# The second image of the late pairs leaves by GpSimd's queue

## The chip, the core and the metric

The kernel runs on one core of a Trainium2 chip. Its time is device microseconds of one execution. A profile is one execution recorded by the hardware profiler; its span runs from the first instruction to the last, on one clock for all engines.

## What is computed

A 3x3 convolution with dilation 2 and zero padding over 16 images of 64 channels and 64x64 pixels, to 128 channels, in float32. The reference, cut to its core:

```python
batch, c_in, h, w, c_out, k, dilation = 16, 64, 64, 64, 128, 3, 2
pad = ((k - 1) * dilation + 1) // 2
x_pad = np.pad(x, ((0, 0), (0, 0), (pad, pad), (pad, pad)))
output[b, co] += weight[co, ci, kh, kw] * x_pad[b, ci, kh*dilation:kh*dilation+h, kw*dilation:kw*dilation+w]
```

An image comes in as 1.05 MB of float32 and goes out as 2.10 MB.

## The kernel before

**Pairs.** The images are worked two at a time. `x_pair` puts the 64 channels of both images of a pair on the 128 partitions, so a pair is one load of 2.10 MB. There are `NP` = 8 pairs, `pb` = 0 to 7. The output tile `o` of a pair holds 128 output channels on the partitions and both images beside each other, 4.19 MB.

**Loads.** Pair 0 comes as float32 by SyncE's queue (L75) into a tile from the pool of the output tiles, and is cast to f16 by the engines. Pairs 1 to 7 are loaded by `load` (L81) on GpSimd's queue, which casts to f16 on the way: 2.10 MB are read, 1.05 MB written. Pairs 1 to 4 are asked for at the start. Pairs 5, 6 and 7 are asked for in the loop over pairs, two pairs ahead (L195, `AHEAD` = 5).

**Sums.** The kernel spares matmuls by working rows that lie two apart together: of four rows (`e`, `r`), rows with `e` = 0 and `e` = 1 share the middle tap, which is applied to their sum. `prepare` (L141) makes these sums `s16` on GpSimd, in two pieces for each pair: at the second and the third step (`u` = 1, 2) of the pair before. The pool of sums has three buffers, so GpSimd waits until PE has read the sums of three pairs earlier.

**Matmuls.** Each pair has `NU` = 4 steps `u` of 16 output rows. A step has three phases, each in its own PSUM tile (four buffers): the middle tap on the sums, copied to `s32` by ScalarE (L204), and one phase for each `e`, which VectorE (DVE) adds to `s32` into `o` (L209).

**Stores.** The pool of output tiles has three buffers, and its first one serves pair 0's float32 load, so the tile of pair `pb` takes the buffer of pair `pb` - 3, and DVE's first add of a pair waits until the store of that pair has landed. All stores leave by SyncE's queue (SP): pairs 0 to 4 as one DMA of 4.19 MB (L221), pairs 5 and 6 as one DMA for each image (L224), and pair 7 in two halves of rows with one DMA for each image. Each store waits for DVE's last add into what it takes.

**Order.** The schedule is written by hand: every engine and every queue keeps the order of the code. An instruction of GpSimd that waits holds all that stands behind it on GpSimd, sums and DMA requests alike.

Of the kernel before, what the change touches and what calls it, by code (L numbers as in the profile page):

```python
# [10 lines left out]
def kernel(  # L11
# [7 lines left out]
    nc = tc.nc  # L19

    B, CI, H, W = x.shape
# [8 lines left out]
    NP = B // 2  # L30
# [47 lines left out]
    def load(pb, cuts):  # L78
        x16[pb] = x16pool.tile([P, H, W], f16, tag="x16", name=f"x16_{pb}")
        for lo, hi in zip(cuts, cuts[1:]):  # L80
            nc.gpsimd.dma_start(out=x16[pb][:, lo:hi], in_=x_pair[pb, :, lo:hi])  # L81

    AHEAD = 5
# [16 lines left out]
    for name, a in (("w21", 2), ("w01", 0)):  # L100
        for u in range(2):
            eng = nc.vector if name == "w21" else nc.gpsimd
            eng.tensor_sub(  # L103
                out=w16[:, SLOT[name] * KW : (SLOT[name] + 1) * KW, u, :],
# [8 lines left out]
    for n, name in enumerate(("w1", "w21", "w0", "w01", "w2")):  # L113
        ps = cpool.tile([P, 2, NB], f32, tag="ps", name=f"wt{n}")
        k0 = SLOT[name] * KW
        for j in range(KW):
            nc.tensor.matmul(  # L117
                out=ps[:, 0, j * CO : (j + 1) * CO],
# [16 lines left out]
    def prepare(pb, lo, hi):  # L135
        if pb not in s16:
            s16[pb] = sumpool.tile([P, 2 * NQ, W], f16, tag="s16", name=f"s16_{pb}")
        src = (x16[pb] if pb else x32).rearrange("p (q e r) w -> p q e (r w)", e=2, r=2)
        dst = s16[pb].rearrange("p (q r) w -> p q (r w)", r=2)
        q0, q1 = lo // 4, hi // 4  # L140
        nc.gpsimd.tensor_add(  # L141
            out=dst[:, q0:q1], in0=src[:, q0:q1, 0, :], in1=src[:, q0:q1, 1, :]
        )
# [37 lines left out]
    def phase(pb, u, terms):  # L181

        ps = cpool.tile([CO, 2, NB], f32, tag="ps", name="ps")
        for pair in zip(*(conv(pb, hb, ps[:, hb], u, terms) for hb in range(2))):
            for m in pair:
                nc.tensor.matmul(**m)  # L186
        return ps

    BOTH = NP - 3
    for pb in range(NP):  # L190
        o = opool.tile([P, 2, H, W], f32, tag="o", name=f"o{pb}")
        ov = o.rearrange("p b (q e r) w -> p b q e (r w)", e=2, r=2)
        for u in range(NU):

            if u == 1 and AHEAD <= pb + 2 < NP:  # L195
                load(pb + 2, [0, H])
            if pb + 1 < NP:
                if u == 1:
                    prepare(pb + 1, 0, 36)
                elif u == 2:  # L200
                    prepare(pb + 1, 36, H)

            s32 = spool.tile([P, 2, NB], f32, tag="s32", name="s32")
            nc.scalar.copy(out=s32, in_=phase(pb, u, [("w1", 2, 0)]))  # L204
            for e, terms in enumerate(
                ([("w21", 1, 0), ("w0", 1, -1)], [("w01", 0, 0), ("w2", 0, 1)])
            ):
                ps = phase(pb, u, terms)
                nc.vector.tensor_add(  # L209
                    out=ov[:, :, u * UQ : (u + 1) * UQ, e, :],  # L210
                    in0=ps.rearrange("p b (q c) -> p b q c", c=QW),
                    in1=s32.rearrange("p b (q c) -> p b q c", c=QW),
                )

            step = NU // 2 if pb == NP - 1 else NU
            if (u + 1) % step == 0:
                fl = slice((u + 1 - step) * 4 * UQ, (u + 1) * 4 * UQ)
                if pb < BOTH:  # L220
                    nc.sync.dma_start(out=out_pair[pb], in_=o)  # L221
                else:
                    for hb in range(2):
                        nc.sync.dma_start(out=out[2 * pb + hb, :, fl], in_=o[:, hb, fl])  # L224


# [33 lines left out]
```

## Time and profile before

| | |
|---|---|
| time, median of 3 runs | 126.64 us (126.16 to 126.73) |
| span of the profiled execution | 124.3 us |
| own device time of the profiled execution | not listed beside its span; the median is 2.3 us over the span |
| PE busy | 105.2 us, last matmul ends before 111 us |
| DVE, ScalarE, GpSimd busy | 80.8, 39.6, 41.4 us |
| moved by the DMA engines | 43.42 MB, mean 349 GB/s |
| HBM read, written | 17.07 MB, 33.55 MB |
| stores, issue to last landing (median) | 21.6 us (4.19 MB), 12.4 us (2.10 MB), 10.6 us (1.05 MB) |
| loads by GpSimd's queue, issue to last landing (median) | 16.0 us |

The page gives the busy time of each engine in 40 slices of the span (3.1 us each), as a digit of tenths; the line DMA is the mean share of the core's 16 DMA engines, and GB/s what they moved, counted as written. q1 is SyncE's queue, q0 GpSimd's. A timeline's line gives the start, the time taken, engine, line, operation and how many; in brackets stands how long the engine was idle before it and what ended that. A line of the stretches gives each engine's busy time and number of instructions, then the granted clock, the DMA share and GB/s.

### The profile page before, as it was taken

The numbers are of one execution on the slowest core, as the hardware profiler recorded it, in microseconds if no ns is written. First come the engines' busy times: TensorE is split into PE (matmuls) and PEld (weight loads), VectorE is DVE, ScalarE is ACT, GpSimd is POOL, SyncE is SP. The second block draws the span as 40 slices with busy tenths as digits, with TensorE's granted clock in tenths as the row PEclk, the third lists the DMA queues.
The fourth block names the chain that finished last, engine by engine and source line by source line (L and its number), as shares of the span: only waits on it lengthen the run. The fifth ranks groups of instructions, "written<-read, shape, count | busy, mean of one in ns | idle before, by whom it ended". The sixth has DMA issues, their size and how long they took to land.

```text
span 124.3 us, 2244 instructions
## 1 busy us (share of the span) xinstructions
PE 105.2 (85%) x981; PEld 55.7 (45%) x981; DVE 80.8 (65%) x71; ACT 39.6 (32%) x40; POOL 41.4 (33%) x33
## 2 busy tenths in 40 slices
PE   6357999999999999999999999999999999960000
PEld 2043555555555555555555555555555555520000
DVE  0470199787778777877769778777877787770000
ACT  4760823333333333333333333333332433320000
POOL 2859998794095009500930093000000000000000
PEclk9999999999999999999999999999999999999655
DMA  4999999999999999999999999999999999999991
GB/s 129 346 359 218 214 214 216 224 237 411 393 327 314 332 306 319 316 390 314 324 345 427 425 427 432 422 427 427 432 438 427 432 414 432 427 417 419 422 406 71
DMA packets 3961, 43.42 MB, mean 349 GB/s; under 512 B 368, under 2 KB 368, under 8 KB 624
## 3 DMA queue, kind: packets, MB, share of 16 engines
q1 hardware_dynamic: 2944, 35.95, 68.9%
q0 software_dynamic: 1008, 7.34, 28.4%
q8 instruction: 7, 0.11, 0.3%
q14 instruction: 2, 0.02, 0.0%
HBM read 17.07 MB, written 33.55 MB: 407 GB/s over the span
## 4 chain that ended last, share of the span: by engine, by line
PE 80%; DMA 5%; POOL 2%; DVE 1%; DVEq 1%; SPq 0%; issue 0%
PE ps L186 80%; DMA x<-in_x_dram 5%; POOL s L141 2%; DVE o L209 1%; DVEq L255 1%; SPq L64 0%; DVEq L209 0%
## 5 line engine op out<-in xcount | busy, mean ns | idle before, releaser
L209 DVE TENSOR_TENSOR o<-ps,s 128x1024 f32<-128x1024 f32 x64 | 76.7, 1223 | 25.9 <-PE ps L186 16.8
L186 PE MATMUL ps<-x,w_sb 64*128 64x496 f16 (+3 forms) x768 | 85.3, 368 | 0.0
L186 PEld LDWEIGHTS <-w_sb 64*128 64x128 f16 x960 | 53.4, 95 | 49.3 <-issue 3.7
L204 ACT COPY s<-ps 128x1024 f32<-128x1024 f32 x32 | 32.4, 1012 | 63.0 <-PE ps L186 63.0
L141 POOL TENSOR_TENSOR s<-x 128x1152 f16<-128x1152 f16 (+4 forms) x18 | 35.1, 1971 | 31.1 <-PE ps L186 28.3
L186 PE MATMUL ps<-s,w_sb 64*128 64x496 f16 (+1 forms) x192 | 26.5, 379 | 2.1 <-POOL s L141 2.1
L81 POOL DMA_DIRECT2D x<-in_x_dram x7 | 4.0, 579 | 0.0
L132 ACT CAST x<-x 128x1024 f16<-128x1024 f32 (+1 forms) x3 | 2.8, 973 | 3.4 <-DMA x<-in_x_dram 3.4
L93 PE MATMUL warm<-zero 128*128 128x512 f16 x6 | 2.7, 630 | 1.2 <-DVE zero L87 1.2
L117 PE MATMUL wt<-ident,w 128*128 128x128 f16 x15 | 1.8, 312 | 2.1 <-ACT w L99 2.1
L103 DVE TENSOR_TENSOR w<-w 128x192 f16<-128x192 f32 x2 | 1.5, 800 | 2.5 <-DMA w<-in_weight_dram 2.5
L117 PEld LDWEIGHTS <-w 128*128 128x128 f16 x15 | 1.5, 146 | 3.0 <-ACT w L99 3.0
L99 ACT CAST w<-w 128x576 f16<-128x576 f32 x2 | 2.3, 1222 | 1.6 <-DMA w<-in_weight_dram 1.6
L103 POOL TENSOR_TENSOR w<-w 128x192 f16<-128x192 f32 x2 | 1.9, 951 | 2.4 <-DMA w<-in_weight_dram 2.4
L126 DVE CAST w_sb<-wt 128x384 f16<-128x384 f32 x3 | 1.6, 552 | 1.4 <-PE wt L117 1.4
L93 PEld LDWEIGHTS <-zero 128*128 128x128 f16 x6 | 0.7, 138 | 2.3 <-DVE zero L87 1.2
L99 ACT ACT_TABLE_LOAD x1 | 1.3, 1283 | 0.7 <-PEq L241 0.7
L128 ACT CAST w_sb<-wt 128x384 f16<-128x384 f32 x2 | 1.0, 478 | 1.1 <-PE wt L117 1.1
L130 DVE CAST x<-x 128x1280 f16<-128x1280 f32 x1 | 0.8, 826 | 0.5 <-DMA x<-in_x_dram 0.5
L87 DVE MEMSET zero<- 128x256 uint32 x1 | 0.3, 272 | 0.9 <-PEq L241 0.9
masks.py:199 POOL TENSOR_SCALAR_AFFINE_SELECT ident<-ident 128x128 f16<-128x128 f16 x1 | 0.3, 292 | 0.1
masks.py:197 POOL MEMSET ident<- 128x128 f16 x1 | 0.2, 204 | 0.3 <-POOLq L241 0.3
(4 smaller groups left out, 0.4 us busy)
## 6 DMA issues: line engine op xcount, KB each, us to landing
out_dram<-o SPq DMA_DIRECT2D x5, 4096.0 KB, 21.6
out_dram<-o SPq DMA_DIRECT2D x4, 2048.0 KB, 12.4
x<-in_x_dram POOLq DMA_DIRECT2D x7, 1024.0 KB, 16.0
out_dram<-o SPq DMA_DIRECT2D x4, 1024.0 KB, 10.6
x<-in_x_dram SPq DMA_DIRECT2D x1, 1152.0 KB, 6.5
x<-in_x_dram SPq DMA_DIRECT2D x1, 896.0 KB, 10.6
w<-in_weight_dram SPq DMA_DIRECT2D x1, 288.0 KB, 2.9
```

What stands on the lines that cost most here:

```text
L81: nc.gpsimd.dma_start(out=x16[pb][:, lo:hi], in_=x_pair[pb, :, lo:hi])
L93: nc.tensor.matmul(out=warm[:, 0], lhsT=zero[:, 0:P], rhs=zero, start=True, stop=True)
L99: nc.scalar.copy(out=w16[:, 0:NK, u, :], in_=w32k)
L103: eng.tensor_sub(out=w16[:, SLOT[name] * KW : (SLOT[name] + 1) * KW, u, :], in0=w32k[:, a * KW : (a + 1) * KW, :], in1=w32k[:, KW : 2 * KW ...
L117: nc.tensor.matmul(out=ps[:, 0, j * CO : (j + 1) * CO], lhsT=w16[:, k0 + j, :, :].rearrange("o t i -> o (t i)"), rhs=ident, start=True, st ...
L126: nc.vector.tensor_copy(out=dst, in_=ps[:, 0, 0 : KW * CO])
L132: nc.scalar.copy(out=x16[0][:, lo:hi], in_=x32[:, lo:hi])
L141: nc.gpsimd.tensor_add(out=dst[:, q0:q1], in0=src[:, q0:q1, 0, :], in1=src[:, q0:q1, 1, :])
L186: nc.tensor.matmul(**m)
L204: nc.scalar.copy(out=s32, in_=phase(pb, u, [("w1", 2, 0)]))
L209: nc.vector.tensor_add(out=ov[:, :, u * UQ : (u + 1) * UQ, e, :], in0=ps.rearrange("p b (q c) -> p b q c", c=QW), in1=s32.rearrange("p b ( ...
L255: with _tile.TileContext(nc) as tc:
```

## The change

Pair 4 (the fifth) leaves as two DMAs, one for each image, as pairs 5 to 7 do. Of each such two, the first image's DMA stays on SyncE's queue, and the second's goes to GpSimd's. The load of pair 7 is taken out of its place in pair 5 and asked for in pair 4, behind the sums for pair 5.

```diff
-    BOTH = NP - 3
+    PAIRED = NP - 4
     for pb in range(NP):
...
-            if u == 1 and AHEAD <= pb + 2 < NP:
+            if u == 1 and AHEAD <= pb + 2 < NP - 1:
                 load(pb + 2, [0, H])
             if pb + 1 < NP:
                 if u == 1:
                     prepare(pb + 1, 0, 36)
                 elif u == 2:
                     prepare(pb + 1, 36, H)
+                    if pb == PAIRED:
+                        load(NP - 1, [0, H])
...
-                if pb < BOTH:
+                if pb < PAIRED:
                     nc.sync.dma_start(out=out_pair[pb], in_=o)
                 else:
-                    for hb in range(2):
-                        nc.sync.dma_start(out=out[2 * pb + hb, :, fl], in_=o[:, hb, fl])
+                    for hb, eng in enumerate((nc.sync, nc.gpsimd)):
+                        eng.dma_start(out=out[2 * pb + hb, :, fl], in_=o[:, hb, fl])
```

GpSimd's order from the sums of pair 5 on, before: load of pair 7, sums of pair 6, sums of pair 7. After: load of pair 7, store of pair 4's second image, sums of pair 6, store of pair 5's, sums of pair 7, store of pair 6's, two stores of pair 7's. The number of instructions on PE, DVE and ScalarE is the same.

## The prediction, made before the changed kernel ran

> **What bounds the kernel now.** I read the page's slices first, because the chain of waits ends at 112.01 us (1.13 us of DVE's own queue after 110.88) while the span ends at 124.3 us. Whatever fills the last 12 us is not in that chain.
>
> ```profile
> PE   6357999999999999999999999999999999960000
> ...
> DMA  4999999999999999999999999999999999999991
> GB/s 129 346 359 218 214 214 216 224 237 411 393 327 314 332 306 319 316 390 314 324 345 427 425 427 432 422 427 427 432 438 427 432 414 432 427 417 419 422 406 71
> ...
> q1 hardware_dynamic: 2944, 35.95, 68.9%
> q0 software_dynamic: 1008, 7.34, 28.4%
> ```
>
> PE looks full for most of the span, but it stops three slices before the end. The DMA engines are at 9 in every slice except the first and the last. So the transfers set the end. The low GB/s figures in slices 4 to 20 are the loads: they write f16 and read twice as many bytes, which the next view, by stretches, lets me compare.
>
> ```profile
> core 0: us, PE busy (x) PEld busy (x) DVE busy (x) ACT busy (x) POOL busy (x), PEclk, DMA share, GB/s
> 14.00:24.00 10.00, 10.00 (x100) 5.42 (x97) 7.98 (x7) 4.03 (x5) 9.30 (x5) 1.00 1.02 214
> 36.00:48.00 12.00, 12.00 (x120) 6.37 (x118) 9.19 (x9) 4.05 (x4) 4.35 (x4) 1.00 1.01 315
> 76.00:112.00 36.00, 34.66 (x336) 18.20 (x332) 28.30 (x24) 11.13 (x11) 0.00 (x0) 1.00 1.01 429
> 118.00:120.00 2.00, 0.00 (x0) 0.00 (x0) 0.00 (x0) 0.00 (x0) 0.00 (x0) 0.50 1.03 434
> 120.00:122.00 2.00, 0.00 (x0) 0.00 (x0) 0.00 (x0) 0.00 (x0) 0.00 (x0) 0.50 0.68 287
> 122.00:124.00 2.00, 0.00 (x0) 0.00 (x0) 0.00 (x0) 0.00 (x0) 0.00 (x0) 0.50 0.05 20
> ```
>
> From 14 to 24 us only GpSimd's queue (q0) moves data: 214 GB/s written, so 428 GB/s read. From 76 to 112 only SyncE's queue (q1) does: 429 GB/s. From 36 to 48 both do; the DMA view of that stretch gives 1.27 MB for q0 and 2.49 MB for q1, so 2.54 + 2.49 MB at the f32 side in 12 us, 419 GB/s, and 48 to 60 gives 434. One queue, the other, or both: the engines move the f32 side at the same pace. An image of 2.10 MB costs 2.10 MB / 429 GB/s = 4.9 us of all sixteen engines, whoever asks for it.
>
> That gives the whole time. In the trace's landing records (one time for each of the sixteen engines) the second piece of x's first pair lands from 8.6 to 12.3 us. After it come 7 loads and 16 images out, 23 x 4.87 us = 112.0 us. For the fastest engine 8.6 + 112.0 = 120.6, and its last landing is at 120.9; the slowest lands at 123.4, and the span closes 0.9 us later. So the fastest engine idles for 0.3 us in 112, and that is all that better order can take, except for the uneven finish (120.9 to 123.4).
>
> **The change part by part.** Now the queues' own clocks, from the timelines of SP and GpSimd:
>
> ```profile
> 74.93 0.37 SPq L221 DMA_DIRECT2D out_dram<-o  x1
> 87.30 1.51 SPq L224 DMA_DIRECT2D out_dram<-o  x2
> 112.04 1.63 SPq L224 DMA_DIRECT2D out_dram<-o  x2
> ...
> 50.73 0.57 POOL L81 DMA_DIRECT2D x<-in_x_dram  x1
> 58.95 4.21 POOL L141 TENSOR_TENSOR s<-x 128x1152 f16<-128x1152 f16 x2 [7.65 <-PE ps L186]
> 71.31 4.21 POOL L141 TENSOR_TENSOR s<-x 128x1152 f16<-128x1152 f16 x2 [8.14 <-PE ps L186]
> ```
>
> *The eighth pair's load.* Before, it stands on GpSimd behind both sums of pair 5 and ahead of the sums of pair 6, and leaves at 50.73. After, it stands in the same place in GpSimd's order, with the new store behind it. Cost 0. Had it stayed at its place in the loop, it would stand behind a store that waits until 74.9.
>
> *One DMA more.* The fifth pair (pair 4 counted from 0) leaves as two DMAs and not one: 16 more completion packets (the page's 368 under 512 B are 16 for each of 23 issues), one per engine, some 10 ns each in the packet records. Cost 0.01 us.
>
> *SP.* It loses one issue of each later group. The second issue of a group takes 1.1 to 1.4 us (1.51 to 1.75 for the two). Nothing gains by it: a store issued at 87.30 lands after some 11 to 16 us, of which its own transfer is 4.9; it stands in the engines' backlog. Gain 0.
>
> *GpSimd.* It gains five store issues at 0.54 to 0.70 us each (the loads' durations; I take 0.57, the median of L81). What is queued behind each matters. The first waits for DVE at 74.93, and the sums of pair 6, which ran at 58.95, now run from 75.5 to 79.7. PE first reads them at 85.74: cover 6.0 us. The second waits until 87.30, and the sums of pair 7, which ran at 71.31, end at 87.30 + 0.57 + 4.21 = 92.1. PE first reads them at 98.11: cover 6.0 us. Cost 0; without that cover each would hold PE.
>
> On whether GpSimd can write its store requests while DVE is busy: the load at 50.73 took 0.57 us with a DVE add running (50.65 to 53.09), the three loads at 9.84 took 0.54 to 0.57 with DVE nearly idle. So DVE's adds cost such a request nothing. The Trainium skill (SBUF — State Buffer, section SBUF: two separate sides) says that a DVE operation in a two-port mode keeps GpSimd from writing descriptors until it ends. By that rule a store would be late by at most one add, 1.22 us, which the 6.0 us cover; these rows show no such hold.
>
> *Who lands when.* At 74.93 SP's queue still has all of pair 3 (landing before at 62.56 + 21.6 = 84.2). The new store of pair 4's second image shares the engines with it from then on, so pair 3 lands 4.87 us later, at 89.0, or 89.4 if the next store (87.3) cuts in. Pair 6's output tile is pair 3's buffer, and DVE first writes it at 87.76: a wait of some 1.6 us. The trace has one such wait:
>
> ```profile
> DVE o L209 <- DMA out_dram<-o: 1.2, 1, 1.2
> ...
> 63.76 4.87 DVE L209 TENSOR_TENSOR o<-ps,s 128x1024 f32<-128x1024 f32 x4 [1.23 <-DMA out_dram<-o]
> ```
>
> After it DVE ran four adds without a gap, PE never stopped, and the next adds came at 69.37, on the regular grid. DVE's gap is 0.75 us in each 3.17, so 1.6 us are made up in about 7 us, inside pair 6's 12.4. Then pair 4's first image, behind pair 3 and beside two stores of the other queue, lands at 84.2 + 3 x 4.87 = 98.8 (before: 74.93 + 18.9 = 93.8); pair 7 first writes that buffer at 100.13. Cover 1.3 us. If it is gone, DVE is late by what is missing, and the end is not: at 112.04, when the last stores are issued, the engines are busy with earlier ones until 115.9 (fastest) to 118.5 (slowest). The start of a DMA takes about 1.6 us (weights: issued 0.74, first landing 3.01, 0.7 of it transfer), so the fastest engine has 2.3 us of cover, the slowest 4.9.
>
> *The end.* From 98.8 on q1 holds 3 images and q0 2, in all 5 x 4.87 = 24.35 us: 123.15 against 123.4 before. q0 is through at about 120.5 and q1's last half image goes alone, as now.
>
> *What a store costs by q0.* The trace has none. Nearest are q0's loads: 8 packets per engine, 4.87 us per 2.10 MB read, the same as q1's stores (96.4 to 101.3 for an image). I take the same. From below: nothing in the rows lets a packet go faster, 0. From above: if rows of 16 KB were cut in pieces of 4 KB (from 309 ns for 8 KB and 611 for 16 KB a packet has some 7 ns of its own, so 4 KB takes 158), 4 x 158 = 632 against 611, +3.4% on 4 x 4.87 us, or +0.7 us. The loads' bytes written give a far bound, 214 GB/s: another 19.5 us; but those packets read 16 KB each, and that explains their time.
>
> Sum: 0 + 0.01 + 0 = 0 on a span of 124.3 us. The profiled execution's own device time is not listed beside its span; the median of the runs, 126.64, lies 2.3 us over the span, and I keep that. Forecast 126.6 us. About 0.5% (0.63 us) is what a measurement of this kernel can tell from no change.
>
> **The rivals.** *Slower: the sixteen engines lose time on q0's stores.* Engines are full, so each lost percent of q0's 19.5 us goes straight to the end; it decides from +3.3% per packet on (0.63 us). Against it: the equal pace of loads and mixed stretches. For it: no store by this queue is in the trace, and in 24 to 31 us, with q1's first store coming in, the slowest engine's landings of two successive loads are 24.4 and 30.7, 6.2 us apart and not 4.9, 1.35 more. Priced from 0.7 (cut rows) to 4 x 1.35 = 5.4 us; I take 1.5: 128.1. The Trainium skill (DMA: Bandwidth & Descriptors, section Latency and other measured facts) calls two of the sixteen engines usually slower, and guesses at GpSimd's descriptor rings as the cause; from 13.4 to 24.4 us, under q0 alone, the spread of a load's sixteen landings is 1.3, 1.25 and 1.3 us and does not grow.
>
> *Slower: GpSimd's queue holds the sums.* If a store held GpSimd until it lands (about 86 us), the sums of pair 6 would end at 90.3 and not 79.7, PE would be 4.6 us late, and the last stores too; over 2.3 us of cover that costs 2.3 us: 128.9. Against it: GpSimd went on 0.57 us after each load, 16 us before it landed.
>
> *Faster: an even finish.* In the last two rows 0.68 x 2 + 0.05 x 2 = 1.46 us of mean work are left at 120; evenly shared, the end comes at 121.5 and not 122.4 to 123.4, about 1 to 1.3 us sooner: 125.5. For it: two queues could shift work between engines. Against it: rows stay with their engine if both queues deal them out alike, and the spread stayed at 2.3 to 2.6 us in all stores from 96 us on.
>
> *The change does not do what it says.* GpSimd's order holds the five stores where the loop puts them; it is as good as excluded, and would give 126.6.
>
> **How the numbers follow.** Forecast, with the excluded case: 0.66. Engines losing time on q0: 0.15. Sums held: 0.06. Even finish: 0.13. So faster 0.13, same 0.66, slower 0.21. The forecast's own range is 126.1 to 127.2; to hold 8 in 10 it reaches to 125.8 and 128.1, which takes in the +0.7 of cut rows and about half of the first and the last rival.
>
> **What would show it.** Right: DMA at 9 to the same slice, an f32 side near 429 GB/s from 76 us on, q0's image at some 4.9 us of engine time, sums of pairs 6 and 7 at 75.5 and 87.9, a DVE wait of about 1.6 us for a store at pair 6 and none or a small one at pair 7, PE ending near 110.3. Wrong: q0's share per byte above q1's by over 3%; a DMA slice under 9 between 75 and 118; PE waiting for GpSimd's sums; landings of the last store spread by much less or more than 2.5 us.

## The result, and the profile after

The changed kernel took 127.62 us (median of 6 runs, 127.25 to 128.64) against 126.60 before: a ratio of 1.0101 with the 95% interval [1.0076, 1.0125] (the two medians alone give 1.0081). Measured three more times beside the kernel before, on three chips, it gave 1.0045 [1.0020, 1.0069], 1.0048 [1.0024, 1.0072] and 1.0056 [1.0039, 1.0073]. So it is slower, by about half a percent in three measurements and by one percent in the first. The forecast was 126.6 us, no change, with a range of 125.8 to 128.1 that holds 127.62; but it put the cost of the change at nothing, and the change costs.

The profile after is of a run of 128.64 us, the slowest of the six. First its slices and queues, on the page:

```profile
span 126.6 us, 2246 instructions
...
DMA  4999999999999999999999999999999999999950
GB/s 129 373 332 220 217 212 212 212 272 424 355 303 336 334 316 329 311 388 313 316 349 440 422 419 435 430 435 419 419 435 430 432 409 424 430 414 430 422 212 8
...
q1 hardware_dynamic: 2240, 27.56, 52.4%
q0 software_dynamic: 1728, 15.73, 43.5%
```

8.4 MB moved from q1 to q0, and the engines are as full as before: no slice under 9 between the first and the last two. By stretches, the pace is the forecast's, and the finish is not:

```profile
core 0: us, PE busy (x) PEld busy (x) DVE busy (x) ACT busy (x) POOL busy (x), PEclk, DMA share, GB/s
76.00:112.00 36.00, 35.46 (x344) 18.45 (x340) 28.03 (x24) 11.21 (x12) 10.64 (x8) 1.00 1.00 426
120.00:122.00 2.00, 0.00 (x0) 0.00 (x0) 0.00 (x0) 0.00 (x0) 0.00 (x0) 0.50 0.84 352
122.00:124.00 2.00, 0.00 (x0) 0.00 (x0) 0.00 (x0) 0.00 (x0) 0.00 (x0) 0.50 0.12 49
124.00:126.00 2.00, 0.00 (x0) 0.00 (x0) 0.00 (x0) 0.00 (x0) 0.00 (x0) 0.50 0.02 8
```

426 GB/s against 429. In this run one engine of the sixteen worked on alone at the end: the last store's landings are at 125.32 for it and 123.27 for the next one. The three other profiles of the changed kernel do not show that (the last two landings lie 0.3 to 1.1 us apart).

GpSimd's and DVE's timelines show the steps between:

```profile
76.00 0.54 POOL L226 DMA_DIRECT2D out_dram<-o  x1 [23.89 <-DVE o L211]
76.55 4.21 POOL L141 TENSOR_TENSOR s<-x 128x1152 f16<-128x1152 f16 x2
88.37 0.58 POOL L226 DMA_DIRECT2D out_dram<-o  x1 [7.60 <-DVE o L211]
88.96 4.21 POOL L141 TENSOR_TENSOR s<-x 128x1152 f16<-128x1152 f16 x2
```

```profile
88.67 2.36 DVE L211 TENSOR_TENSOR o<-ps,s 128x1024 f32<-128x1024 f32 x2 [0.60 <-DMA out_dram<-o]
```

A store costs GpSimd 0.54 to 0.58 us, the sums of pair 6 follow at once and end 5.8 us before PE reads them (80.76 against 86.54), and pair 6's first add waits 0.60 us for pair 3's store. The last lines of interest are those of the program's close, the queue instructions behind the last store, before and after. EVENT_SEMAPHORE is a wait for counters; a counter is raised when a DMA has landed. GpSimd's long DRAIN starts when its last work is issued and in these traces ends only after that work is done.

```profile
L255 SPq EVENT_SEMAPHORE  x11: 17/28/28, 113.7 to 124.2; - x11
L255 POOLq DRAIN  x3: 39/93/4854, 71.3 to 124.0; - x3
L255 SPq DRAIN  x3: 7/7/7, 123.4 to 123.7; - x3
```

```profile
L257 SPq EVENT_SEMAPHORE  x11: 17/28/5092, 113.2 to 126.6; - x11
L257 POOLq DRAIN  x3: 45/93/12767, 113.1 to 126.3; - x3
L257 SPq DRAIN  x3: 7/7/7, 125.7 to 126.1; - x3
```

The columns are the shortest, median and longest duration in ns and the first and last start. Before, GpSimd's long drain was over at 71.3 + 4.9 = 76.2. After, it starts at 113.1 and takes 12.77 us, to 125.85, 0.53 us past the last landing. SyncE's longest wait, 5.09 us, is for the counter of GpSimd's last store; five waits stand behind it.

### The profile page after: what moved, and what is told of

The parts are those of the page before. It is cut to its first block, busy times and chain, and to the rows that moved or that the text cites. A ratio compares the mean times of both kernels' runs of the same rounds, so it can differ in the third digit from the quotient of the medians.

```text
span 126.6 us, 2246 instructions
## 1 busy us (share of the span) xinstructions
PE 106.5 (84%) x981; PEld 55.5 (44%) x981; DVE 81.0 (64%) x71; ACT 39.6 (31%) x40; POOL 44.2 (35%) x38
## 4 chain that ended last, share of the span: by engine, by line
PE 75%; issue 5%; DMA 5%; POOL 2%; DVE 2%; POOLq 0%; SPq 0%; DVEq 0%
PE ps L186 75%; DMA x<-in_x_dram 5%; DVE o L211 2%; POOL s L141 2%; POOLq L257 0%; POOL out_dram L226 0%; SPq L64 0%; DVEq L211 0%
## 5 line engine op out<-in xcount | busy, mean ns | idle before, releaser
L186 PE MATMUL ps<-x,w_sb 64*128 64x496 f16 (+3 forms) x768 | 86.6, 372 | 0.0
L226 POOL DMA_DIRECT2D out_dram<-o x5 | 2.7, 549 | 50.3 <-DVE o L211 50.3
```

Source lines behind the costliest of these rows:

```text
L226: eng.dma_start(out=out[2 * pb + hb, :, fl], in_=o[:, hb, fl])
```

## The experiments

Each ran beside the kernel before, 12 runs of each version (7 of `late_gpsimd`). The first group was made for four theories of the 1.0 us.

**The change again, three times** (`again`, `again_b`, `again_c`).

> The changed kernel once more, with a second profile. Four theories of the 1.0 us it lost. SOFTWARE: a store asked for by GpSimd costs the DMA engines, or one of them, time that the same store by SyncE does not. TWO QUEUES: any two queues with stores at once do it, whoever owns them. WAITS: images land later, DVE and PE are held, and the last stores are asked for later. END: only the split last stores and what follows their landing cost. All expect 127.6 +- 0.3 us here. SOFTWARE and TWO QUEUES expect one engine to land its last store about 2 us after the others again, as in the first profile (125.3, the next 123.3); if the last landings lie within 2.5 us as before the change, that straggler was chance.

1.0045. The straggling engine did not return: the last two landings are at 123.60 and 123.88, and all sixteen lie within 2.3 us. By the terms set ahead it was chance; what held that engine back was not found. GpSimd's last store is the one that lands last, in all four profiles.

> The changed kernel a third time, beside the controls of this group. CLOSING, a theory formed from the first group: nothing in the stream of stores costs time; the program's close does. SyncE waits at the end for each of 8 counters of its own DMAs in a fixed order, some 60 ns each, and what is still to be waited for once the last store has landed comes on top: 4 here, none before (0.24 us). GpSimd's own drain ends later when it asked for a store last (0.12 us), and the time outside the span grows by 0.24 us. In all +0.6: 127.2 +- 0.15. STREAM, its rival: a second queue or a split store also slows the engines; it expects 127.6, as in the first measurement.

1.0048, 127.12 us, inside CLOSING's range and not at STREAM's 127.6.

> The changed kernel a fourth time, for the half of the first result (1.0101) that the close does not explain. In the profiles so far GpSimd's last store is the one that lands last, its drain ends 0.53 us after that landing, and the span ends 1.30 us after it against 0.89 before the change; with 0.25 us more outside the span that is +0.65 us, 1.0051. CLOSING alone expects 1.005 +- 0.0025 again, and the first result was high by chance or by its chip. STREAM AS WELL expects 1.008 or more.

1.0056. The close alone gives 1.0051. The extra half percent of the first measurement came in none of the three.

**All stores by SyncE** (`all_sync`).

```diff
-                    for hb, eng in enumerate((nc.sync, nc.gpsimd)):
+                    for hb, eng in enumerate((nc.sync, nc.sync)):
```

> The changed kernel with both images of pairs 4 to 7 on SyncE's queue: what is left of the change is the fifth pair in two DMAs and the eighth load's place. SOFTWARE, TWO QUEUES, WAITS and END all expect 126.6 +- 0.2 us, the time before. If the split or the load costs, 127.6.

1.0037 [1.0012, 1.0062], 127.11 us: nearly as much as the change in its repeats, without GpSimd's queue. None of the four theories had said so, and it led to the close:

```profile
L257 SPq EVENT_SEMAPHORE  x11: 17/28/28, 113.9 to 124.9; - x11
L257 SPq DRAIN  x3: 7/7/7, 124.1 to 124.4; - x3
```

The trace's records show SyncE waiting there, after its last store, for the counters of all its DMAs in a fixed order; most of these waits take in one of GpSimd's counters too. When nothing is left to wait for, they follow each other every 0.06 us. SyncE's DMAs take 8 counters in turn. Before, the sixteenth and last DMA has the eighth counter, which is waited for last; here a seventeenth takes the first. It lands at 123.61, and seven waits are left: SyncE's first drain starts 0.52 us after the landing.

**ScalarE's queue in GpSimd's place** (`act_queue`).

```diff
             nc.scalar.copy(out=s32, in_=phase(pb, u, [("w1", 2, 0)]))
+            while later:
+                to, of = later.pop()
+                nc.scalar.dma_start(out=to, in_=of)
...
-                    for hb, eng in enumerate((nc.sync, nc.gpsimd)):
-                        eng.dma_start(out=out[2 * pb + hb, :, fl], in_=o[:, hb, fl])
+                    nc.sync.dma_start(out=out[2 * pb, :, fl], in_=o[:, 0, fl])
+                    later.append((out[2 * pb + 1, :, fl], o[:, 1, fl]))
+                    if pb == NP - 1 and u == NU - 1:
+                        to, of = later.pop()
+                        nc.scalar.dma_start(out=to, in_=of)
```

> The changed kernel with ScalarE's queue in GpSimd's place, asked for behind the copy of the next step so that ScalarE is not held at a pair's end. SOFTWARE expects 126.6 (before), TWO QUEUES and WAITS 127.6 (after), END 127.6 if a second queue at the end is enough, whoever owns it.

1.0054 [1.0029, 1.0079]. SyncE and ScalarE take the eight counters in turn together, again 17 DMAs in all. SyncE's last store has the first counter and lands last, at 124.06 (ScalarE's at 123.85). So seven waits are left, worth 0.43 us (1.0034); the other 0.2 percent lies inside the interval. ScalarE's queue is thus no better than GpSimd's, but the run does not tell the stream from the close.

**The last pair by SyncE** (`last_by_sync`).

```diff
-                    for hb, eng in enumerate((nc.sync, nc.gpsimd)):
+                    second = nc.sync if pb == NP - 1 else nc.gpsimd
+                    for hb, eng in enumerate((nc.sync, second)):
```

> The changed kernel with both images of the last pair on SyncE's queue, pairs 4 to 6 as changed. END expects 126.6. SOFTWARE and TWO QUEUES, if the loss goes with the images by the other queue (3 of 4 left), 127.3; WAITS 127.6, since what holds pairs 6 and 7 is all still there.

1.0014 [0.9988, 1.0040], 126.83 us, with three images still going by GpSimd. END was right in its place; SOFTWARE and TWO QUEUES (127.3) and WAITS (127.6) lie above the interval.

The second group set the close against the stream.

**The kernel before, the first pair's store in two** (`first_split`).

```diff
-                if pb < BOTH:
+                if 0 < pb < BOTH:
```

> The kernel before with one thing changed: the first pair's store leaves as two DMAs, one for each image, both by SyncE. Its last store thereby takes the first counter of eight and not the last. CLOSING expects 7 waits of 60 ns behind the last landing, +0.43 us: 127.0, and nothing outside the span. STREAM expects 126.6: no late pair is touched, and no second queue is used.

1.0039 [1.0011, 1.0067], 126.92 us. The end of the stream is as before (last landing 123.56; before 123.37), and the close is longer, though all that changed lies almost 100 us ahead of it:

```profile
L255 SPq EVENT_SEMAPHORE  x11: 17/28/28, 113.9 to 124.8; - x11
L255 SPq DRAIN  x3: 7/7/7, 124.1 to 124.4; - x3
```

SyncE's first drain starts 0.51 us after the last landing here and 0.08 us after it before.

**Only the last pair's second images by GpSimd** (`last_by_gpsimd`).

```diff
-                    for hb in range(2):
-                        nc.sync.dma_start(out=out[2 * pb + hb, :, fl], in_=o[:, hb, fl])
+                    second = nc.gpsimd if pb == NP - 1 else nc.sync
+                    for hb, eng in enumerate((nc.sync, second)):
+                        eng.dma_start(out=out[2 * pb + hb, :, fl], in_=o[:, hb, fl])
```

> The kernel before with only the second images of the last pair (two DMAs of 1.05 MB) on GpSimd's queue. CLOSING expects 2 waits (0.12) + GpSimd's drain (0.12) + 0.24 outside the span = +0.48: 127.05. STREAM, with 1 image of 4 by that queue, expects a quarter of its 1.0: 126.85, with the time outside the span as before.

1.0013 [0.9988, 1.0038], 126.84 us, 1.77 us outside the span: the time is 0.2 us less than CLOSING said, and just what STREAM said. CLOSING's two terms for GpSimd were tied to GpSimd asking last, and here GpSimd's store landed at 122.66, 1.1 us before SyncE's (123.76):

```profile
L256 POOLq DRAIN  x3: 45/93/10761, 112.3 to 124.5; - x3
L256 SPq DRAIN  x3: 7/7/7, 124.0 to 124.3; - x3
```

GpSimd's drain ended at 123.07, before SyncE had signalled. So the reading is that GpSimd's terms cost only where its store lands last; what is left of CLOSING is two waits, and the span's end does lie 0.12 us further behind the landing. This was seen after the run, and the run does not decide between the two theories.

**Stores in packets of 8 KB** (`rows_8k`), for the uneven finish.

```diff
-    BOTH = NP - 3
+    BOTH = NP - 4
...
-            step = NU // 2 if pb == NP - 1 else NU
+            step = NU // 2 if pb >= BOTH else NU
```

> The kernel before with pairs 4 to 6 stored as pair 7 is, in halves of rows, so in packets of 8 KB and not 16, all by SyncE. In the packet records one engine at a time takes 634 to 660 ns for packets of 16 KB from about 70 us on, the others 611; the 8 KB packets take 309 on all. SLOW ENGINE expects the last store's sixteen landings within 1.5 us and not 2.5, and the end 0.5 to 1 us earlier: 125.6 to 126.1. If the slow engine's pace has nothing to do with the size of packets, 126.6 + 0.06 for one wait at the close, and up to +0.3 for the shorter packets.

1.0019 [0.9993, 1.0045]. SLOW ENGINE fell: the 8 KB packets run at 309 ns from 105 us on with none over 342, and the last landings still spread over 2.4 us.

**The change with its close mended** (`close_mended`) and **with only SyncE's counters mended** (`late_gpsimd`).

```diff
-                if pb < PAIRED:
+                if 3 <= pb < PAIRED:
...
-                    for hb, eng in enumerate((nc.sync, nc.gpsimd)):
+                    late = pb == NP - 1 and u == NU - 1
+                    second = nc.sync if pb < PAIRED or late else nc.gpsimd
+                    for hb, eng in enumerate((nc.sync, second)):
```

> The changed kernel's stores of pairs 4 to 6 by two queues and of pair 7's first half too, with the close mended: pair 7's second half leaves by SyncE alone, so GpSimd's last store lands early, and the first three pairs' stores leave as two DMAs each, so that SyncE's last store has the last of its 8 counters. CLOSING expects the time before, 126.55 +- 0.15, and 1.78 us outside the span. STREAM, with 3.5 of 4 images still shared, expects most of the loss, 127.0 or more.

1.0016 [0.9992, 1.0039], 126.32 us against 126.27. Three and a half of the four images still share the engines, and no loss clear of noise is left; STREAM's 127.0 lies above the interval.

```profile
L259 POOLq DRAIN  x3: 45/93/13781, 106.3 to 124.8; - x3
L259 SPq DRAIN  x3: 7/7/7, 124.2 to 124.5; - x3
```

GpSimd's drain is over at 120.03, and SyncE's starts 0.08 us after the last landing (124.14), as before the change.

```diff
-                if pb < PAIRED:
+                if pb < 0:
...
-                    for hb, eng in enumerate((nc.sync, nc.gpsimd)):
+                    second = nc.sync if pb < PAIRED else nc.gpsimd
+                    for hb, eng in enumerate((nc.sync, second)):
```

> The changed kernel with pairs 0 to 3 stored as two DMAs each by SyncE, so that SyncE's last store has the last counter (no wait of 60 ns left behind it), and GpSimd still asks for pair 7's last store. CLOSING expects what is left of its sum: 0.12 for GpSimd's drain + 0.24 outside the span, 126.9, with 2.03 us outside. STREAM expects 127.1 or more, as with the change whole.

1.0073 [1.0047, 1.0100], 127.41 us, 2.03 us outside: CLOSING had the outside right and the sum too low, 0.36 us where 0.9 [0.6, 1.3] were measured. The mended counters were SyncE's, and the store that lands last (124.05) is GpSimd's: its counter is still waited for ahead of others, and its drain still ends 0.53 us after the landing. The close measured here is 0.42 us in the span and 0.25 outside, and that sum the interval holds.

The closes side by side, from the landing records of each profile, the means over all runs of the time outside the span, and the ratios:

| kernel | lands last | waits left behind it | span's end after last landing, us | outside the span, us | ratio |
|---|---|---|---|---|---|
| before | SyncE | 0 | 0.89 | 1.78 | 1 |
| close_mended | SyncE | 0 | 0.89 | 1.79 | 1.0016 |
| rows_8k | SyncE | 1 | 0.96 | 1.80 | 1.0019 |
| last_by_sync | SyncE | 2 | 1.02 | 1.77 | 1.0014 |
| last_by_gpsimd | SyncE | 2 | 1.01 | 1.77 | 1.0013 |
| act_queue | SyncE | 7 | 1.32 | 1.77 | 1.0054 |
| all_sync | SyncE | 7 | 1.33 | 1.78 | 1.0037 |
| first_split | SyncE | 7 | 1.32 | 1.78 | 1.0039 |
| the change, four profiles | GpSimd | 5, and GpSimd's drain | 1.30 to 1.31 | 2.03 to 2.04 | 1.0045 to 1.0101 |
| late_gpsimd | GpSimd | 5, and GpSimd's drain | 1.31 | 2.03 | 1.0073 |

In the change's own profile the five waits bring SyncE's signal to 0.43 us after the last landing (before: 0.15), and GpSimd's drain ends 0.10 us after that signal. Together they make nearly all of the 0.41 us by which its span ends later.

Did the stream itself end later? An estimate takes from each median the time outside the span and the span's end after the last landing, as measured in that kernel's profile. The last store then lands at 123.7 to 123.8 us in the three repeats, and at 123.6 to 123.9 in the kernel before beside them. So the stream ended no later there, to within 0.1 us. In the first measurement the same sum gives 124.3 against 123.9.

The Trainium skill (DMA: Bandwidth & Descriptors, section Issuing engines are not separate DMA queues) has it that DMAs started by several engines run on the same sixteen and save only the time of issuing. `close_mended` agrees for the stream: 1.0016 with 3.5 images on the second queue.

No version beat the kernel before: what the change cost can be taken away, and these versions found nothing to gain under it.

## Why the prediction was wrong

**What bounds the kernel** held. Engines full, 4.87 us for an image whoever asks, no gain from order.

**The load, the added DMA in the stream, SP's issues, GpSimd's issues and the sums' cover** held: costs of 0, and sums done 5.7 to 5.8 us before they are read, where 6.0 was forecast. GpSimd writes a store's request in 0.53 to 0.58 us whether DVE adds or not (0.57 at 100.81, with an add from 100.93 on; 0.53 at 113.10, with DVE done). The Trainium skill's hold of GpSimd by a DVE operation in a two-port mode (SBUF — State Buffer, section SBUF: two separate sides) does not show with these adds; whether they run in such a mode no run shows.

**Who lands when** held at its end and not in its working. Pair 3's last landing was forecast for 89.0 to 89.4 and was at 88.5 to 88.9 in the first three profiles and at 87.4 in the fourth; DVE's wait was forecast at 1.6 us and was 0.60, 1.02, 1.91 and none; PE did not stop for it, and pair 7 did not wait. But the two queues did not share evenly, as "shares the engines with it from then on" took it. From 78 to 84 us the DMA view of the profile after gives

```profile
q1 hardware_dynamic: 112, 1.77, 69.0%
q0 software_dynamic: 50, 0.82, 31.9%
```

and from 84 to 90 us 50.0 and 49.6. (In `again_b` the shares are 61 and 42, then 60 and 41; what decides them was not found.) So GpSimd's first store, asked for at 76.00, landed at 92.3, and not near 87.3, which half of the engines from 77.6 on (1.6 us for the start) would give.

**What a store costs by q0** held: 611 ns at the median for a packet of 16 KB on either queue in the profile after, where I took the loads' pace. The rival "engines lose time on q0's stores" fell with that, and with `close_mended`.

**The end** is the step that failed first: "q0 is through at about 120.5 and q1's last half image goes alone, as now". It rests on "From 98.8 on q1 holds 3 images and q0 2". With less than its half of the engines early on, q0 was behind that: its second image landed only at 103.2 to 103.7 in the four profiles, while pair 4's first image, forecast for 98.8 on q1, was through at 94.1 to 96.9. So GpSimd's last store landed last in every profile of the change, 0.2 to 0.6 us behind SyncE's, and the close fell to its counter and to GpSimd's drain.

**The sum** failed with it: "lies 2.3 us over the span, and I keep that". Nothing was put down for the close, neither in the span nor outside it. Measured, it is 1.30 - 0.89 = +0.41 us in the span and 2.04 - 1.78 = +0.26 outside: 0.67 us, or 0.5%, which is what the three repeats show. The 2.3 was itself too high: it set the median of the runs against the span of one quick run, 124.26 us, and the mean outside is 1.78. And the "Cost 0.01 us" of one DMA more counted its packets and not its counter: in `first_split` and `all_sync`, where SyncE has one DMA more, the span ends 0.43 us further behind the last landing.

**The even finish** and **the sums held by GpSimd's queue** did not come about.

**What stays open.** The first measurement's other half percent. It lies inside the span, since its six runs have 2.03 us outside as the repeats have. Its profiled run shows one engine two microseconds late, its other five runs have no profile, and three repeats on three chips did not have it. What makes up the 0.26 us outside the span is not in a profile; it comes wherever GpSimd's store lands last, and in no other kernel here.

## What to carry to other kernels

Here the transfers are the bound, and handing stores to another queue moved no time in the stream. In such a kernel the sum should go on past the last landing: who waits for the last DMA, in which order, and what each issuing engine does before the program may end. Let the store that lands last have the counter that is waited for last, and let it not be GpSimd's; the number of DMAs ahead of it decides which counter it gets. A difference of half a percent can sit in the close of a program and look like an effect of its stream, so compare the last landing with the span's end before looking for it elsewhere.

## What the runs showed of the hardware

- The close waits for the DMA counters at 0.06 us each: 0, 1, 2 and 7 waits left gave 0.89, 0.96, 1.01 to 1.02 and 1.32 to 1.33 us from the last landing to the span's end.
- GpSimd's drain behind its last store ended 0.41 to 0.53 us after that store's landing, in all kernels where GpSimd stored. Where that store was the last of all, the time outside the span was 2.03 to 2.04 us and not 1.77 to 1.80.
- Two queues with stores at once took 69 and 32 percent of the engines' time in one stretch and 50 and 50 in the next, at an unchanged total of 426 to 431 GB/s (the profile after, 78 to 84 and 84 to 90 us).
